# First stage of a two-layer trunk kernel in eight steps of 128 features, with x asked for first

## The chip, the core and the metric

The kernel runs on one core of a Trainium2 chip. The metric is device microseconds (us) of one execution of the whole kernel; it has one launch and no arithmetic on the host. The engines are called by their names or as the profile abbreviates them: TensorE (PE, its weight loads PEld), VectorE (DVE), ScalarE (ACT), GpSimd (POOL) and SyncE (SP), which issues most DMAs. Each engine works through its own queue in order.

## The reference

The kernel computes two layers of a streaming encoder on x of 512 tokens by 1024 features, in float32. Layer 0 mixes by retention (4 heads, 256 wide queries and keys, 512 wide values, chunks of 64), layer 1 by chunked attention (16 heads of 128). Ahead of each layer stands a normalisation with a shift, a scale and a gate that come from a conditioning vector c:

```
def rms_norm_f32(t, gain):
    return t32 * lax.rsqrt(jnp.mean(t32 * t32, axis=-1, keepdims=True) + EPS) * gain
...
m = silu(c) @ ada_w[l] + ada_b[l]         # 3 x 1024 values: shift, scale, gate
h = rms_norm_f32(x, norm_g[l]) * (1 + scale) + shift
...
proj = h @ w_in                           # layer 0: q, k, v, g in its columns
q, k = apply_rope(q, cos, sin), apply_rope(k, cos, sin) * (RET_QK_DIM ** -0.5)
o = retention(q, k, v), normalised per head, * silu(g)
x = x + gate * (o @ w_out)
```

The lines on m, h, o and x are cut to what they compute. For the change it matters that h, of 512 x 1024, needs three things: the root of the mean square of each token (a sum over all 1024 features), and one shift and one scale per feature, each a dot of 1024 products of silu(c) with a column of ada_w.

## The kernel before, in words

Matrix products are made in three passes: each operand is split in a high half (rounded to the type that TensorE multiplies) and a low half (what is left), and high x high, high x low and low x high are summed in PSUM. The split of weights is an ACT copy to the high half (`whi`, L222) and a DVE subtraction to the low half (`wlo`, L223); that of h and of others is `split` (L305 to L308). h is held with features on partitions, as `hTh` and `hTl`, in eight blocks of 128 features.

**Start.** SP asks for cond (c on all partitions), then the four tiles of x (`norm_x`, L360). Per tile `norm_rows` makes sums of squares on ACT (L168), adds them on DVE (L174), makes the root on POOL in two operations (`rstd_of`, L117 and L119) and scales the rows (L181 on DVE, for the last tile L179 on ACT). TensorE transposes the result and ACT copies it to `xT` (L369).

**First stage.** The products that the first stage makes are those of the values of head 0 (`rv0`, 512 columns of ret_w_in, four PSUM tiles `pm_rv`, one per 128 tokens) and of its queries (`rqk0_0`, 256 columns, two tiles `pm_rqk`). It runs in four steps of 256 features. `prepare(s)` asks for two 1 MB pieces of ada_w (`ada_256`), makes four dots of 1024 on DVE (L124), adds the constant parts for two features' blocks at a time (`ada_finish`), makes h on DVE (L379), splits it, and loads and splits 256 rows of the weights. The matmuls of step s come behind `prepare(s + 1)`.

**Hand-over.** Its last step is followed by the evacuation of the values (`vh` on ACT, `vl` on DVE, L306 and L307), the keys of head 0 (`rqk0_2`, weights in two halves of 512 features, `whi_rqk_2` and `wlo_rqk_2`), and the tables of sines (`rope_tables`: positions and the frequencies `tiny` are loaded through POOL's queue, the angle is made on DVE, L431 to L448). The tiles of this part lie in the pool `rp`, which is opened when the first stage's pool `st` is closed, in the same memory. `zero` (L408) is a block of zeros in it.

**The rest of layer 0.** The work is cut in units of twelve matmuls; `go` counts them in `now`, and `at(u, ...)` hangs a piece of other work behind unit u. So are the gate's eight dots hung (blocks 16 to 23 of ada_w: `side_load`, `side_dot`, L601 to L605). Behind the fourth and the eighth `ada_finish` turns four dots into 512 values of the gate: a diagonal block each (`diag`), four small matmuls that spread them to all partitions (`gp`, L146), and a copy to `gate` on ACT (L148). The output projection of head 0 (`outp`, `out_proj`) needs them: its weights `raw_r` are multiplied by a half of the gate on POOL (L219) before they are split, first half for `po_r_0`, second for `po_r_1`. `hang_scores` hangs the scores of the next head (`st`, L520).

The program is written in this order, and a scheduler with its own costs places the instructions on the engines' queues; loads and dots marked with `keep_in_program_order` keep their order among themselves. All later placing in the two kernels is the same from the second head on.

## Time and profile before

| what | us |
|---|---|
| median of three runs | 980.64 (980.63 to 984.66) |
| profiled execution | 982.98 |
| its span, from the first to the last instruction | 981.2 |
| TensorE busy | 949.3 (97%) |
| VectorE busy | 601.1 (61%) |
| ScalarE busy | 373.8 (38%) |
| GpSimd busy | 184.7 (19%) |
| mean granted clock of TensorE | 0.992 of full speed |

The span is shorter than the time of its execution by what lies around the instructions. Busy times of engines overlap. A share of the span is an average over stages: in the first of forty slices of the span TensorE is busy for three tenths, in the second for eight, and from the third on for nine or more, while the DMA engines are at nine tenths in the first slice and between two and six in nearly all others. So the stretch that the change touches is unlike the rest.

### The profile page before, as it was taken

How to read it: one execution, taken by the hardware profiler on the slowest of the kernel's cores; microseconds unless marked ns; L12 is line 12 of the kernel's file. 1: busy time of each engine (PE TensorE's matmuls, PEld its weight loads, DVE VectorE, ACT ScalarE, POOL GpSimd, SP SyncE). 2: the span in 40 equal slices, each digit the busy share in tenths (PEclk: the TensorE clock that was granted, in tenths of full speed). 3: DMA queues.
4: the chain of work that ended last, by engine and by line, in shares of the span. 5: the costliest groups of instructions: out<-in, count | busy, mean ns of one | idle time of the engine just before them, and what ended most of it. 6: DMA issues, size and time to landing. Idle time of an engine off the chain costs nothing.

```text
span 981.2 us, 11783 instructions
## 1 busy us (share of the span) xinstructions
PE 949.3 (97%) x4528; PEld 793.6 (81%) x4528; DVE 601.1 (61%) x1023; ACT 373.8 (38%) x785; POOL 184.7 (19%) x169
## 2 busy tenths in 40 slices
PE   3889999999999999999999999999999999999997
PEld 2778888888888888778788888888878888888886
DVE  4977796568544775864455557444676346555674
ACT  6233322232233233354444445233543244444441
POOL 3000520051002012503001250002520012004410
PEclk8899999999999999999999999999999999999999
DMA  9654436434443433312333213223212232223202
GB/s 352 241 191 160 149 99 204 151 108 140 150 150 108 150 100 104 97 57 80 101 97 97 79 62 103 91 87 96 97 58 93 87 97 90 79 70 99 95 1 86
DMA packets 70296, 111.76 MB, mean 114 GB/s; under 512 B 11888, under 2 KB 36512, under 8 KB 70240
## 3 DMA queue, kind: packets, MB, share of 16 engines
q1 hardware_dynamic: 58256, 103.29, 31.5%
q0 software_dynamic: 10832, 5.62, 2.1%
q10 hardware_dynamic: 1152, 2.10, 0.6%
q8 instruction: 35, 0.57, 0.2%
q14 instruction: 21, 0.17, 0.1%
HBM read 108.83 MB, written 2.10 MB: 113 GB/s over the span
## 4 chain that ended last, share of the span: by engine, by line
PE 86%; DMA 4%; issue 4%; DVE 3%; ACT 1%; POOL 1%; SPq 0%; POOLq 0%; ACTq 0%; DVEq 0%
PE pm_aqk L233 5%; PE pm_aqk L231 5%; PE pm_aqk L232 5%; PE po_a L231 3%; PE po_a L233 3%; PE po_a L232 3%; PE pm_av L232 3%; PE pm_av L233 3%; PE pm_rg L239 3%; PE pm_rg L240 3%; PE ao L765 3%; PE as L725 3%; PE pm_av L231 3%; PE pm_rg L241 3%; PE ro L540 3%
## 5 line engine op out<-in xcount | busy, mean ns | idle before, releaser
L231 PE MATMUL pm_aqk<-whi_aqk,hTh 128*128 128x512 f32 x256 | 102.3, 400 | 1.1 <-ACT hTh L200 1.1
L233 PE MATMUL pm_aqk<-whi_aqk,hTl 128*128 128x512 f32 x256 | 100.4, 393 | 0.0
L232 PE MATMUL pm_aqk<-wlo_aqk,hTh 128*128 128x512 f32 x256 | 100.2, 391 | 0.0
L124 DVE CUSTOM_DVE_ANT_0 ada<-ada,cond 128x1024 f32<-128x1024 f32 x48 | 63.3, 1332 | 1.7 <-DMA ada<-in_ada_t_dram 1.7
L219 POOL TENSOR_TENSOR raw_r<-raw_r,gate 128x2048 f32<-128x2048 f32 x8 | 38.2, 4771 | 106.3 <-DMA raw_r<-in_ret_w_out_dram 92.9
L231 PE MATMUL pm_rv<-whi_rv,hTh 128*128 128x512 f32 x128 | 51.2, 407 | 6.7 <-ACT hTh L306 6.7
L231 PEld LDWEIGHTS pm_aqk<-whi_aqk,hTh 128*128 128x128 f32 x256 | 48.1, 188 | 10.9 <-ACT hTh L200 1.5
L233 PEld LDWEIGHTS pm_aqk<-whi_aqk,hTl 128*128 128x128 f32 x256 | 48.1, 188 | 10.6 <-DVE hTl L201 0.4
L232 PEld LDWEIGHTS pm_aqk<-wlo_aqk,hTh 128*128 128x128 f32 x256 | 48.2, 188 | 9.2
L734 ACT ACTIVATE p<-p,nm 128x128 f32<-128x128 f32 (+1 forms) x64 | 35.9, 563 | 48.7 <-DVE nm L732 47.6
L223 DVE TENSOR_TENSOR wlo_aqk<-raw_aqk,whi_aqk 128x2048 fp32r<-128x2048 f32 x16 | 36.6, 2290 | 28.0 <-ACT whi_aqk L222 28.0
L728 DVE CUSTOM_DVE_ANT_0 p<-as,br 128x128 f32<-128x128 f32 (+1 forms) x64 | 30.4, 486 | 36.9 <-PE as L725 34.0
L241 PE MATMUL pm_rqk<-hTh,wlo_rqk 128*128 128x512 f32 x128 | 49.7, 391 | 2.5 <-DVE wlo_rqk L223 2.5
L713 POOL DMA_DIRECT2D br<-in_att_bias_dram x16 | 13.4, 839 | 204.4 <-DVE nm L732 168.8
L232 PE MATMUL pm_rv<-wlo_rv,hTh 128*128 128x512 f32 x128 | 50.9, 402 | 0.0
L239 PE MATMUL pm_ag<-hTh,whi_ag 128*128 128x512 f32 x128 | 50.7, 397 | 0.0
L240 PE MATMUL pm_ag<-hTl,whi_ag 128*128 128x512 f32 x128 | 50.5, 394 | 0.0
L231 PE MATMUL po_r<-whi_r,yh 128*128 128x512 f32 x128 | 49.8, 391 | 0.5 <-ACT whi_r L222 0.5
L241 PE MATMUL pm_ag<-hTh,wlo_ag 128*128 128x512 f32 x128 | 50.2, 395 | 0.0
L233 PE MATMUL po_r<-whi_r,yl 128*128 128x512 f32 x128 | 50.1, 392 | 0.0
L232 PE MATMUL po_r<-wlo_r,yh 128*128 128x512 f32 x128 | 50.0, 391 | 0.0
L231 PE MATMUL pm_av<-whi_av,hTh 128*128 128x512 f32 x128 | 50.0, 391 | 0.0
(199 smaller groups left out, 2548.6 us busy)
## 6 DMA issues: line engine op xcount, KB each, us to landing
ada<-in_ada_t_dram SPq DMA_DIRECT2D x32, 512.0 KB, 4.4
raw_aqk<-in_att_w_in_dram SPq DMA_DIRECT2D x32, 512.0 KB, 4.6
ada<-in_ada_t_dram SPq DMA_DIRECT2D x8, 1024.0 KB, 13.8
raw_rg<-in_ret_w_in_dram SPq DMA_DIRECT2D x8, 1024.0 KB, 5.1
raw_r<-in_ret_w_out_dram SPq DMA_DIRECT2D x8, 1024.0 KB, 5.0
raw_ag<-in_att_w_in_dram SPq DMA_DIRECT2D x8, 1024.0 KB, 5.2
raw_av<-in_att_w_in_dram SPq DMA_DIRECT2D x8, 1024.0 KB, 5.1
raw_a<-in_att_w_out_dram SPq DMA_DIRECT2D x8, 1024.0 KB, 4.9
```

What stands on the lines that cost most here:

```text
L124: return nc.vector.tensor_tensor_reduce(raw, raw, cond, 1.0, 0.0, ALU.mult, ALU.add, mod[:, layer, block : block + 1])
L219: nc.gpsimd.tensor_tensor(raw, raw, scale.unsqueeze(1).broadcast_to([P, k1 - k0, width]), ALU.mult)
L223: nc.vector.tensor_tensor(lo, raw, f32(hi), ALU.subtract)
L231: nc.tensor.matmul(ps, a_h, wh[:, k, :], start=first and k == 0, stop=False)
L232: nc.tensor.matmul(ps, a_h, wl[:, k, :], start=False, stop=False)
L233: nc.tensor.matmul(ps, a_l, wh[:, k, :], start=False, stop=last and k == 3)
L239: nc.tensor.matmul(ps, wh[:, k, csl], h, start=first and k == 0, stop=False)
L240: nc.tensor.matmul(ps, wh[:, k, csl], l, start=False, stop=False)
L241: nc.tensor.matmul(ps, wl[:, k, csl], h, start=False, stop=last and k == 3)
L540: nc.tensor.matmul(ps[:, S - w :], a[:, fsl], b[:, psl], start=j == 0 and z == 0, stop=j == 3 and z == 2,)
L728: nc.vector.tensor_tensor_reduce(p[:, :w], ps[:, :w], br[:, S - w :], 1.0, -3.0e38, ALU.add, ALU.max, mx)
L734: nc.scalar.activation(p[:, :w], p[:, :w], AF.Exp, bias=nm, accum_out=sm)
```

## The change

The first stage becomes eight steps of 128 features. A step asks for one 1 MB load (a block of the scale's and one of the shift's rows of ada_w) and two small ones of the first weights (512 and 256 columns of 128 rows, 256 KB and 128 KB), makes two dots on DVE, the scale on DVE and the shift on POOL, h on ACT in place of DVE, and splits it and the weights. The weights' split halves lie in whole tiles for all steps, those of the queries in the pool `st`. x is asked for first, cond behind its third tile. The sums of squares of tiles 1 and 3 are made on DVE, and the scaled rows of the last tile too. A tiny Silu at the start stands ahead of the one on cond. The loads of `rqk0_2` keep their program order. The eight dots of the gate are hung at other units.

```diff
--- before.py
+++ after.py
@@ -73,8 +73,11 @@
     pa = ctx.enter_context(tc.tile_pool(name="pa", bufs=4, space=PS))
 
     cond = cp.tile([P, D], F32, name="cond")
-    nc.sync.dma_start(cond, c_row.broadcast_to([P, D]))
     xs = [cp.tile([P, D], F32, name=f"x_{t}") for t in range(NT)]
+    for t in range(NT):
+        nc.sync.dma_start(xs[t], x[t * P : (t + 1) * P, :])
+        if t == 2:
+            nc.sync.dma_start(cond, c_row.broadcast_to([P, D]))
     ng = cp.tile([P, 2, NK], F32, name="ng")
     nc.gpsimd.dma_start(ng, norm_t)
     bt = cp.tile([P, 2, 24], F32, name="bt")
@@ -92,11 +95,15 @@
     nc.vector.memset(ones, 1.0)
     ones_r = cp.tile([P, P], F32R, name="ones_r")
     nc.vector.tensor_copy(ones_r, ones)
     nc.gpsimd.memset(mhalf, -0.5)
 
+    tick = cp.tile([P, 8], F32, name="tick")
+    nc.vector.memset(tick, 0.0)
     with tc.high_priority():
-        nc.scalar.activation(cond, cond, AF.Silu)
+        nc.scalar.activation(tick, tick, AF.Silu)
+    nc.scalar.activation(cond, cond, AF.Silu)
     kq = cp.tile([P, 1], F32, name="kq")
     nc.vector.tensor_scalar(kq, qg, kg, float(P**-0.5), ALU.mult, ALU.mult)
 
@@ -160,25 +167,25 @@
         return sums
 
 
-    def norm_rows(t, tag, scalar=False):
+    def norm_rows(t, tag, vector=False):
 
         xn, ss = [], sp.tile([P, 2], F32, tag="ss", name=f"ss_{tag}_{t}")
         for half in range(2):
             xh = np_.tile([P, 512], F32, tag="p", name=f"xn_{tag}_{t}_{half}", bufs=6)
-            nc.scalar.activation(
-                xh, xs[t][:, half * 512 : (half + 1) * 512], AF.Square,
-                accum_out=ss[:, half : half + 1],
-            )
+            src = xs[t][:, half * 512 : (half + 1) * 512]
+            if vector:
+                nc.vector.tensor_tensor_reduce(
+                    xh, src, src, 1.0, 0.0, ALU.mult, ALU.add, ss[:, half : half + 1]
+                )
+            else:
+                nc.scalar.activation(xh, src, AF.Square, accum_out=ss[:, half : half + 1])
             xn.append(xh)
         s1 = sp.tile([P, 16], F32, tag="s1", name=f"s1_{tag}_{t}")
         nc.vector.tensor_tensor(s1[:, 0:1], ss[:, 0:1], ss[:, 1:2], ALU.add)
         rs = rstd_of(s1[:, 0:1], D, 1)
         for half in range(2):
             src = xs[t][:, half * 512 : (half + 1) * 512]
-            if scalar:
-                nc.scalar.activation(xn[half], src, AF.Copy, scale=rs)
-            else:
-                nc.vector.tensor_scalar(xn[half], src, rs, None, ALU.mult)
+            nc.vector.tensor_scalar(xn[half], src, rs, None, ALU.mult)
         return xn
 
     def norm_tile(layer, t):
...
@@ -258,7 +267,7 @@
             self.w = load(
                 [(d, self.w_in[rows, c0 : c0 + d.stop - d.start]) for d, c0 in self.cols],
                 f"{self.name}_{half}", self.width, w=self.w if ks[0] else parts,
-                k0=ks[0], k1=ks[-1] + 1,
+                k0=ks[0], k1=ks[-1] + 1, pinned=self.name == "rqk0_2",
             )
 
         def unit(self, half, u, ks=range(4)):
@@ -348,54 +357,56 @@
     with tc.tile_pool(name="st", bufs=1) as st:
         xT = st.tile([P, NK, S], F32, name="xT")
 
...
+        wv = [[wp.tile([P, 4, 512], F32R, tag=a, name=f"{a}_rv0_{z}") for a in ("whi", "wlo")] for z in range(2)]
+        wq = [[st.tile([P, 4, 256], F32R, name=f"{a}_rqk0_0_{z}") for a in ("whi", "wlo")] for z in range(2)]
+        bt1 = st.tile([P, NK], F32, name="bt1")
+        nc.gpsimd.tensor_scalar(bt1, bt[:, 0, NK : 2 * NK], 1.0, None, ALU.add)
+        for t in range(NT):
+            xn = norm_rows(t, 0, t % 2 == 1)
+            for half in range(2):
+                ps = pa.tile([P, 4, P], F32, tag="pa", name=f"hp_0_{t}_{half}")
+                for k in range(4):
+                    nc.tensor.transpose(ps[:, k, :], xn[half][:, k * P : (k + 1) * P], ident)
+                nc.scalar.activation(
+                    xT[:, half * 4 : half * 4 + 4, t * P : (t + 1) * P], ps, AF.Copy
+                )
+        rows = ada_t[0, : 2 * D].rearrange("(g q p) k -> q p g k", g=2, q=NK)
+        def prepare(kt):
+            raw = st.tile([P, 2, D], F32, tag="ada", name=f"ada_0_{kt}", bufs=4)
+            tc.keep_in_program_order(nc.sync.dma_start(raw, rows[kt]))
+            rw = st.tile([P, 768], F32, tag="rw", name=f"rw_{kt}", bufs=4)
+            ksl = slice(kt * P, (kt + 1) * P)
+            nc.sync.dma_start(rw[:, :512], ret_w_in[ksl, 2 * D : 2 * D + 512])
+            nc.sync.dma_start(rw[:, 512:], ret_w_in[ksl, 0:256])
+            ada_dot(raw[:, 1, :], 0, NK + kt)
+            g1, s1 = gs[:, 0, kt : kt + 1], sh[:, 0, kt : kt + 1]
+            nc.vector.scalar_tensor_tensor(
+                g1, mod[:, 0, NK + kt : NK + kt + 1], bt1[:, kt : kt + 1], ng[:, 0, kt : kt + 1],
+                ALU.add, ALU.mult,
             )
...
+            ada_dot(raw[:, 0, :], 0, kt)
+            nc.gpsimd.tensor_tensor(s1, mod[:, 0, kt : kt + 1], bt[:, 0, kt : kt + 1], ALU.add)
+            half, k = divmod(kt, 4)
+            for (hi, lo), src in ((wv[half], rw[:, :512]), (wq[half], rw[:, 512:])):
+                split(hi[:, k, :], lo[:, k, :], src)
+            h = np_.tile([P, S], F32, tag="nat", name=f"h_0_{kt}")
+            nc.scalar.activation(h, xT[:, kt, :], AF.Identity, bias=s1, scale=g1)
+            split(hT["h"][:, kt, :], hT["l"][:, kt, :], h)
+        def products(kt):
+            for ch, w in zip(first, (wv, wq)):
+                ch.w = (None, *w[kt // 4])
+                for u in range(ch.n):
+                    ch.unit(kt // 4, u, range(kt % 4, kt % 4 + 1))
         prepare(0)
...
+        for kt in range(NK - 1):
+            prepare(kt + 1)
+            products(kt)
 
     offs = (0, 512, 896, 1152)
 
@@ -600,15 +611,14 @@
         blocks = [(0, 16 + b) for b in range(8)]
         blocks += [(1, b) for b in (*range(8, 16), *range(8), *range(16, 24))]
         for z, (layer, block) in enumerate(blocks):
-            u = 2 + 2 * z if z < 8 else 20 + (z - 8) * 7 // 2
+            u = 5 + 3 * z // 2 if z < 8 else 20 + (z - 8) * 7 // 2
             at(max(u - 4, 0), side_load, layer, block)
             at(u, side_dot, layer, block)
 
         rope_tables()
         for ch, ev in zip(first, (v_evac(0), qk_evac(0))):
             ch.evac = ev
-            for u in range(ch.n):
-                ch.unit(1, u, range(2, 4))
+        products(NK - 1)
         go(Chunk("rqk0_2", ret_w_in, [(h256, D)], True, qk_evac(0, 2)).units())
         hang_scores(0, now[0] + 2)
         for n in range(RH):
```

TensorE's queue around the last matmuls of the second gate half (`gp_20`, columns 512 to 1023 of the gate) in the kernel before. `po_r_0` and `po_r_1` are the two column halves of the first output projection, `st` the scores of the next head:

```order
L146 MATMUL gp_20_992<-diag_22_999,ones 128x128
L231 MATMUL po_r_0_0_1109<-whi_r_0_1103,yh_1_854 128x512
L232 MATMUL po_r_0_0_1109<-wlo_r_0_1104,yh_1_854 128x512
L146 MATMUL gp_20_992<-diag_23_1002,ones 128x128
L233 MATMUL po_r_0_0_1109<-whi_r_0_1103,yl_1_855 128x512
L231 MATMUL po_r_0_0_1109<-whi_r_0_1103,yh_2_893 128x512
...
L520 MATMUL st_1_1182<-qh_1_1053,kl_1_1098 128x384
L231 MATMUL po_r_1_0_1200<-whi_r_1_1194,yh_0_818 128x512
L520 MATMUL st_2_1214<-qh_0_1048,kh_0_1092 128x256
...
L231 MATMUL po_r_1_1_1225<-whi_r_1_1194,yh_0_818 128x512
...
L231 MATMUL po_r_1_2_1252<-whi_r_1_1194,yh_0_818 128x512
L232 MATMUL po_r_1_0_1200<-wlo_r_1_1195,yh_0_818 128x512
```

And in the changed kernel:

```order
L242 MATMUL po_r_0_3_1205<-whi_r_0_1140,yl_3_973 128x512
L153 MATMUL gp_20_1016<-diag_20_1017,ones 128x128
L531 MATMUL st_0_1194<-qh_0_1085,kh_0_1129 128x512
L153 MATMUL gp_20_1016<-diag_21_1020,ones 128x128
...
L531 MATMUL st_2_1251<-qh_1_1090,kl_1_1135 128x256
L153 MATMUL gp_20_1016<-diag_22_1023,ones 128x128
L153 MATMUL gp_20_1016<-diag_23_1026,ones 128x128
L531 MATMUL st_3_1278<-qh_0_1085,kh_0_1129 128x256
...
L531 MATMUL st_3_1278<-qh_1_1090,kl_1_1135 128x256
L240 MATMUL po_r_1_0_1237<-whi_r_1_1231,yh_0_854 128x512
...
L240 MATMUL po_r_1_3_1304<-whi_r_1_1231,yh_0_854 128x512
L241 MATMUL po_r_1_0_1237<-wlo_r_1_1232,yh_0_854 128x512
```

In before the last `gp_20` stands inside the first unit of `po_r_0`; now it stands behind the whole of `po_r_0` and the first three blocks of scores, and the first `po_r_1`, with `whi_r_1`, is seven instructions behind it.

ScalarE's queue at the end of the first stage in the kernel before, with the semaphores that each instruction waits for; `vh` is the high half of the values, `whi_rqk_2_0` the first half of the keys' weights:

```order
L306 ACTIVATE hTh_111<-h_7_401 128x512 [waits DVE_49]
L306 ACTIVATE vh_490<-pm_rv_0_277 128x512 [waits DMAHW6_49,DMAHW5_49,DMAHW7_49,DMAHW0_49,PE_49]
L306 ACTIVATE vh_490<-pm_rv_1_284 128x512 [waits PE_49]
L306 ACTIVATE vh_490<-pm_rv_2_291 128x512 [waits PE_49]
L306 ACTIVATE vh_490<-pm_rv_3_298 128x512 [waits PE_49]
L222 ACTIVATE whi_rqk_2_0_549<-raw_rqk_2_0_548 128x4x256 [waits DMAHW5_49,Activation_49]
L222 ACTIVATE whi_rqk_2_1_588<-raw_rqk_2_1_587 128x4x256 [waits DMAHW0_49,DVE_49,PE_49]
```

And in the changed kernel:

```order
L315 ACTIVATE hTh_118<-h_7_480 128x512 [waits Activation_49]
L315 ACTIVATE vh_542<-pm_rv_0_268 128x512 [waits DMAHW2_49,DMAHW7_49,DVE_49,PE_49]
L315 ACTIVATE vh_542<-pm_rv_1_272 128x512
L315 ACTIVATE vh_542<-pm_rv_2_276 128x512
L315 ACTIVATE vh_542<-pm_rv_3_280 128x512
L231 ACTIVATE whi_rqk_2_0_586<-raw_rqk_2_0_585 128x4x256 [waits DMAHW5_49]
L231 ACTIVATE whi_rqk_2_1_622<-raw_rqk_2_1_621 128x4x256 [waits DMAHW0_49]
```

The first `vh` waits for loads, DVE and TensorE in the changed kernel, since its memory is that of the first stage's pool; the PE event is that of the last matmul of the first stage. The other copies and the keys' weights stand behind it.

GpSimd's queue at the same place in the kernel before:

```order
L119 TENSOR_TENSOR rs<-ms,mhalf 128x1 [waits Pool_49]
L423 DMA posi<-in_positions_dram 128x512 [waits DVE_49]
L408 MEMSET zero 128x128 [waits DMAHW5_49,DMAHW2_49,DMAHW6_49,DMAHW1_49,DMAHW7_49,DMAHW0_49,DVE_49]
L426 DMA tiny<-in_inv_freq_dram 128x1
L427 MEMSET tiny 128x1
```

And in the changed kernel:

```order
L392 TENSOR_TENSOR sh<-mod,bt 128x1 [waits DVE_49] x8
L434 DMA posi<-in_positions_dram 128x512 [waits Activation_49]
L419 MEMSET zero 128x128 [waits DMAHW3_49,DMAHW2_49,DMAHW4_49,DMAHW1_49,DMAHW5_49,DMAHW0_49,DMAHW6_49,DVE_49,DMAHW7_49,PE_49,Activation_49]
L437 DMA tiny<-in_inv_freq_dram 128x1
L438 MEMSET tiny 128x1
```

The block of zeros, which is written into the same memory, now waits for TensorE and ScalarE too, and the load of the frequencies `tiny` stands behind it in both.

## Rows read from the trace of the kernel before

**Rows 1.** The page's busy table, whole span: busy us, share, instructions.
```profile
PE 949.3 (97%) x4528; PEld 793.6 (81%) x4528; DVE 601.1 (61%) x1023; ACT 373.8 (38%) x785; POOL 184.7 (19%) x169
```

**Rows 2.** Waits of TensorE, whole span: line waited for: us in total, times, longest.
```profile
PE pm_rv L231 <- ACT hTh L306: 6.7, 2, 4.0
```

**Rows 3.** Timeline of TensorE: start, us, line, operation, shape, count, idle before.
```profile
17.20 2.21 PE L368 MATMUL hp<-ident,xn 128*128 128x128 f32 x8 [2.63 <-ACT xn L179]
23.42 0.80 PE L231 MATMUL pm_rv<-whi_rv,hTh 128*128 128x512 f32 x1 [4.01 <-ACT hTh L306]
...
62.34 0.39 PE L239 MATMUL pm_rqk<-hTh,whi_rqk 128*128 128x512 f32 x1
...
65.94 0.50 PE L241 MATMUL pm_rqk<-hTh,wlo_rqk 128*128 128x512 f32 x1 [2.52 <-DVE wlo_rqk L223]
...
71.51 0.39 PE L241 MATMUL pm_rqk<-hTh,wlo_rqk 128*128 128x512 f32 x1
```

**Rows 4.** Timeline of VectorE, the start and the first step (same columns).
```profile
9.20 0.88 DVE L181 TENSOR_SCALAR xn<-x,rs 128x512 f32<-128x512 f32 x2 [0.98 <-POOL rs L119]
...
13.48 0.15 DVE L174 TENSOR_TENSOR s<-ss 128x1 f32<-128x1 f32 x1
...
25.42 1.22 DVE L124 CUSTOM_DVE_ANT_0 ada<-ada,cond 128x1024 f32<-128x1024 f32 x1
...
26.57 0.69 DVE L307 TENSOR_TENSOR hTl<-h,hTh 128x512 fp32r<-128x512 f32 x1
27.17 1.22 DVE L124 CUSTOM_DVE_ANT_0 ada<-ada,cond 128x1024 f32<-128x1024 f32 x1
```

**Rows 5.** Timeline of GpSimd, root for the last tile of x.
```profile
14.97 1.42 POOL L119 TENSOR_TENSOR rs<-ms,mhalf 128x1 f32<-128x1 f32 x1
```

**Rows 6.** Timeline of ScalarE at the end of the first stage.
```profile
59.82 0.60 ACT L306 ACTIVATE vh<-pm_rv 128x512 fp32r<-128x512 f32 x1 [0.76 <-PE pm_rv L233]
60.32 1.05 ACT L222 ACTIVATE whi_rqk<-raw_rqk 128x1024 fp32r<-128x1024 f32 x1
```

**Rows 7.** Windows: stretch, us, busy per engine, TensorE's clock, DMA share, GB/s.
```profile
16.90:27.00 10.10, 5.79 (x17) 4.25 (x17) 7.91 (x15) 6.72 (x11) 0.00 (x0) 0.50 1.04 417
...
44.50:47.50 3.00, 3.00 (x7) 2.42 (x8) 3.00 (x6) 1.49 (x3) 0.00 (x0) 0.50 0.00 0
...
63.40:66.00 2.60, 0.07 (x2) 0.06 (x1) 2.60 (x5) 0.00 (x0) 0.00 (x0) 1.00 0.00 0
```

**Rows 8.** DMA issues, first 70 us: count, KB each, median us to landing.
```profile
ada<-in_ada_t_dram SPq DMA_DIRECT2D x8, 1024.0 KB, 13.8
...
kg<-in_att_kg_t_dram POOLq DMA_DIRECT2D x1, 0.5 KB, 5.6
tiny<-in_inv_freq_dram POOLq DMA_DIRECT2D x1, 0.5 KB, 7.0
```

**Rows 9.** Timeline of VectorE, angle and second low weights.
```profile
56.16 0.49 DVE L431 TENSOR_SCALAR ang<-posf,tiny 128x512 f32<-128x512 f32 x1
...
59.06 0.43 DVE L440 TENSOR_SCALAR n<-ang 128x512 f32<-128x512 f32 x1
...
64.66 1.22 DVE L223 TENSOR_TENSOR wlo_rqk<-raw_rqk,whi_rqk 128x1024 fp32r<-128x1024 f32 x1
```

**Rows 10.** Timeline of GpSimd, gate times raw_r.
```profile
105.37 5.59 POOL L219 TENSOR_TENSOR raw_r<-raw_r,gate 128x2048 f32<-128x2048 f32 x1 [1.39 <-ACT gate L148]
...
135.56 4.69 POOL L219 TENSOR_TENSOR raw_r<-raw_r,gate 128x2048 f32<-128x2048 f32 x1 [11.95 <-ACT gate L148]
```

**Rows 11.** Timeline of TensorE, last matmuls of the second gate half.
```profile
134.46 0.38 PE L146 MATMUL gp<-diag,ones 128*128 128x128 f32 x2
```

**Rows 12.** Timeline of ScalarE, gate and high half.
```profile
134.88 0.60 ACT L148 ACTIVATE gate<-gp 128x512 f32<-128x512 f32 x1 [3.34 <-PE gp L146]
...
141.38 1.90 ACT L222 ACTIVATE whi_r<-raw_r 128x2048 fp32r<-128x2048 f32 x1
```

**Rows 13.** Timeline of VectorE, low half.
```profile
146.19 2.28 DVE L223 TENSOR_TENSOR wlo_r<-raw_r,whi_r 128x2048 fp32r<-128x2048 f32 x1
```

More of the change, by code (lines that the diff above doesn't have):

```diff
@@ L94, in hybrid_trunk_kernel @@
     nc.vector.tensor_copy(ones_r, ones)
-    mhalf = cp.tile([P, 40], F32, name="mhalf")
+    mhalf = cp.tile([P, 32], F32, name="mhalf")
     nc.gpsimd.memset(mhalf, -0.5)
+    tick = cp.tile([P, 8], F32, name="tick")
+    nc.vector.memset(tick, 0.0)
     with tc.high_priority():
-        nc.scalar.activation(cond, cond, AF.Silu)
+        nc.scalar.activation(tick, tick, AF.Silu)
+    nc.scalar.activation(cond, cond, AF.Silu)
     kq = cp.tile([P, 1], F32, name="kq")
@@ L201, in norm_tile, with load @@
             nc.vector.tensor_tensor(hT["l"][:, ksl, tsl], h, f32(hT["h"][:, ksl, tsl]), ALU.subtract)
-    def load(parts, name, width=512, scale=None, w=None, k0=0, k1=4):
+    def load(parts, name, width=512, scale=None, w=None, k0=0, k1=4, pinned=False):
         if w is None:
@@ L349, in hybrid_trunk_kernel @@
         xT = st.tile([P, NK, S], F32, name="xT")
-        def ada_256(b0):
-            raw = st.tile([P, 2, D], F32, tag="ada", name=f"ada_0_{b0}", bufs=6)
-            nc.sync.dma_start(
-                raw, ada_t[0, b0 * P : (b0 + 2) * P, :].rearrange("(b p) k -> p b k", p=P)
-            )
-            for j in range(2):
-                ada_dot(raw[:, j, :], 0, b0 + j)
-            ada_finish(0, b0, 2)
-        def norm_x():
-            for t in range(NT):
-                nc.sync.dma_start(xs[t], x[t * P : (t + 1) * P, :])
-            for t in range(NT):
-                xn = norm_rows(t, 0, t == 3)
-                for half in range(2):
-                    ps = pa.tile([P, 4, P], F32, tag="pa", name=f"hp_0_{t}_{half}")
-                    for k in range(4):
-                        nc.tensor.transpose(ps[:, k, :], xn[half][:, k * P : (k + 1) * P], ident)
-                    nc.scalar.activation(
-                        xT[:, half * 4 : half * 4 + 4, t * P : (t + 1) * P], ps, AF.Copy
-                    )
@@ L373, in prepare @@
-        def prepare(s):
-            ada_256(NK + 2 * s)
-            ada_256(2 * s)
-            for kt in (2 * s, 2 * s + 1):
-                h = np_.tile([P, S], F32, tag="nat", name=f"h_0_{kt}")
-                nc.vector.tensor_scalar(
-                    h, xT[:, kt, :], gs[:, 0, kt : kt + 1], sh[:, 0, kt : kt + 1], ALU.mult, ALU.add
-                )
-                split(hT["h"][:, kt, :], hT["l"][:, kt, :], h)
-            for ch in first:
-                ch.load(s // 2, ks(s))
-        def ks(s):
-            return range(s % 2 * 2, s % 2 * 2 + 2)
@@ L389, in hybrid_trunk_kernel @@
-        norm_x()
-        prepare(0)
-        for s in range(3):
-            ws = [ch.w for ch in first]
-            prepare(s + 1)
-            for ch, w in zip(first, ws):
-                new, ch.w = ch.w, w
-                for u in range(ch.n):
-                    ch.unit(s // 2, u, ks(s))
-                ch.w = new
+        wv = [[wp.tile([P, 4, 512], F32R, tag=a, name=f"{a}_rv0_{z}") for a in ("whi", "wlo")] for z in range(2)]
+        wq = [[st.tile([P, 4, 256], F32R, name=f"{a}_rqk0_0_{z}") for a in ("whi", "wlo")] for z in range(2)]
@@ L609, in hybrid_trunk_kernel @@
             ch.evac = ev
-            for u in range(ch.n):
-                ch.unit(1, u, range(2, 4))
+        products(NK - 1)
         go(Chunk("rqk0_2", ret_w_in, [(h256, D)], True, qk_evac(0, 2)).units())
```

4 lines of the change are left out of this document (3 added, 1 removed).

## Prediction, made before the changed kernel was timed

> **What bounds the kernel now.** I read the busy table first: TensorE is busy for 949.3 us of the span [rows 1], so a change pays only by removing TensorE's idle time, and costs only by adding some. Then the list of TensorE's waits, and TensorE's timeline over the first 150 us to see where these waits lie. The reader is to see two things. The idle time that this change can reach lies ahead of 66 us: after the transposes of x the first matmul comes at 23.42, 4.01 late; a second wait for h takes the other 2.7 us of its 6.7, and a third gap of 2.52 ends at 65.94, when the low half of the third weights is ready [rows 2, 3]. The first stage is over at 62.34, when the next chunk's first matmul starts [rows 3]. Of the 32 us that TensorE is idle in all, the start and these gaps are most, so behind 66 us there is little slack: whatever the first stage gains reaches the end of the kernel unless a new wait eats it.
>
> Sums are made against the profiled execution (982.98, its span 981.2, so 1.8 around it); it is 2.34 above the median of the runs, 980.64. I apply differences to the median. Half a per cent, 4.9 us, is what a measurement here can tell from no change: 975.74 and 985.54 are the bounds.
>
> **The start.** x is asked for ahead of cond, and two of the four sums of squares move to VectorE. The last tile still goes through GpSimd, whose two tiny operations run beside VectorE's dots: in before the sum of its squares is there at 13.48 and its root at 14.97 + 1.42 = 16.39 [rows 4, 5]. I leave that chain where it is, since x's last tile arrives behind the same bytes as before. Then the two scaled halves (0.88 for two [rows 4], 17.3), transposes and the copy to xT (four transposes, half of the 2.21 of the last eight [rows 3], and a copy of 0.6 [rows 6]: 1.7), then h and its high half on ScalarE at 0.6 each [rows 6]: 20.2 for the first matmul, 3.2 ahead of 23.42. What goes is that four dots had to be over before h; now two have.
>
> **The eight steps.** A step is 18 matmuls. At the full clock they start 0.227 apart (24 from 65.94 to 71.51, the first of them 0.11 slow [rows 3]), so 4.08 a step. VectorE in a step: two dots 1.15 apart, three low halves (two of 512 at 0.60, one of 256, half of that), a small one of 0.1 [rows 4]: 2.3 + 1.5 + 0.1 = 3.9. ScalarE: h, its high half and two weights, 2.2. GpSimd: one small addition, which I bound by nothing and by 1.42, the worst of its small operations beside dots [rows 5]; it is hidden, as the steps are prepared one ahead. Loads: 1.44 MB at the 417 GB/s of the stretch from 16.9 to 27 [rows 7] is 3.4. So TensorE sets the pace and the gap of 2.7 in the middle, with its 3.0 us at half clock behind it [rows 7], goes. The half clock at the start stays: it lasted from 23.42 to 27.0 [rows 3, 7]. End of the stage: 20.2 + 3.6 (eight and a half matmuls) + 135.6 x 0.227 = 54.6, against 62.34: 7.7 earlier.
>
> **The hand-over gives part of it back.** The small weights of all eight steps now lie in the pool whose memory the next stage reuses, so the first copy of v and GpSimd's zero block wait for the last matmul of the stage, as the order shows. In before the four copies of v lay beside matmuls. Now: four copies 0.5 apart and then the high weights, 1.05 [rows 6], TensorE idle from 54.6 to about 57.95, with 0.2 for the release. Queued behind GpSimd's zero block is the load of the frequencies: issued at 54.95, landing 5.6 to 7.0 later (the shortest and this load's own in before [rows 8]). VectorE's angle operation waits for it, and the second low weights stand behind five operations of the angle: 3.3 in before, from 56.16 to 59.49, then 1.15 to 1.22 [rows 9]. They are ready at 65.0 to 66.4, I take 65.7. TensorE gets to their first use 28 matmuls after 57.95 plus a short wait for the first low half: 64.6 at the full clock, 66.1 with 3.0 us at half clock as after the gap of 2.7 [rows 7]. That gap of 2.52 was followed by full clock [rows 7], this one is 3.35, so I take the half: 66.1. In before the same matmul starts at 71.51 [rows 3]. What is left is 5.4 us; ends 4.9 and 6.9.
>
> **The second half of the gate.** The unit numbers of the eight gate dots change, and with them the place at which the last matmul of the second gate half stands. In before it starts at 134.46; the gate is copied from 134.88, GpSimd scales raw_r from 135.56 for 4.69, the high half starts at 141.38 and takes 1.90, the low half 146.19 and 2.28, done at 148.47 [rows 10 to 13]. TensorE did not notice, because 55 instructions of the output projection and the scores stand between the gate's last matmul and the first that needs the high half, and 14 more ahead of the first that needs the low half. In the changed kernel all of the first projection half stands ahead of the gate; behind it stand only six matmuls of st_3 (256 columns, 0.12 each, half of a 512-column one) and four that need the high half. From the start g of the gate's last matmul: copy at g + 0.42, GpSimd g + 1.1 to 5.8, high half g + 5.9 to 7.8 (in before 1.1 after GpSimd's end, behind another copy), low half to g + 10.1. The matmul that needs it would stand at g + 1.8 without a wait: 8.3 us lost. The low end is 6.0 (if only the wait for the high half counted, 7.8 less 1.8), the high end 9.2: GpSimd took 0.9 longer in the first half of the gate [rows 10]. TensorE stands still for 7.0 of that, so the clock falls; half clock lasted 3.0 and 3.6 us [rows 3, 7], which costs 1.5 to 1.8, of which up to two thirds lie in the shadow of the wait for the low half: 0.5 to 1.7, I take 1.1. Nothing makes this good later, as from there on the order of all engines is the same as before.
>
> Sum: -5.4 + 8.3 + 1.1 = +4.0, so 984.6 (987.0 for the profiled execution).
>
> **Rivals.** (C) The loads become the pace, and it is slower. Each load waits for the landing of the one eight ahead; eight are 2.67 steps, 10.9 us at TensorE's pace. If they take longer than that to land, TensorE waits at every step. For it: the loads of the shift and scale rows took 13.8 us to land [rows 8]. Against it: that was queueing at 417 GB/s with 256 KB loads among them [rows 7, 8], and less is outstanding now. At 13.8 a step takes 5.2, the stage ends at 61.8, and the hand-over takes the rest: 71.51 is missed by about 1.8, so nothing gained and the gate's 9.4 lost, 980.64 + 9.4 = 990.0, or 991.8 at worst. The Trainium skill bears on this one ("DMA: Bandwidth & Descriptors", section "Measured (HBM→SBUF, 128 partitions, SWDGE, issued from GpSimd)"): it says to batch DMAs to at least 1 MiB for 75% of peak, with 341 GB/s for 1 MB against 138 for 64 KB. By it the 384 KB that come in two loads per step would take up to 2.8 us and the 1 MB 3.1, an estimate of 5.9 per step, slower than TensorE. The trace disagrees as far as it goes: 417 GB/s with loads of 256 KB, 512 KB and 1 MB queued together.
>
> (B) The gate's wait isn't there, because something ahead of it on TensorE already waits, or the gap is filled: only the 5.4 stay, 975.3. For it: in before the whole chain lay hidden. Against it: the durations of GpSimd, ScalarE and VectorE [rows 10, 12, 13] leave nothing to choose, TensorE's queue is in order.
>
> (D) The hand-over costs less (the load lands in 5.6 and the clock holds) and the gate's wait has no clock loss behind it: -6.9 + 8.3 = +1.4, 982.0.
>
> **Numbers.** Forecast 0.66, 984.6, its own range 982 to 988; C 0.14, B 0.10, D 0.10. Slower by over 0.5%: 0.25 of the forecast and 0.11 of C, 0.36. Within: 0.41, 0.09 of D, 0.03 of B and 0.03 of C, 0.56. Faster: 0.07 of B and 0.01 of D, 0.08. The range of 8 in 10 leaves out B and the worst of C: 980.0 to 989.5.
>
> **What would show it.** First matmul at 19.5 to 20.7 and no gap before 54; a gap of 3.3 at 54.6 ended by ScalarE's high weights; TensorE at the first use of the second low weights at about 66; one gap of some 7 us near 142 on the first po_r matmul of the second half, released by whi_r, and half clock behind it; after that the same timeline shifted by 4. It is wrong if GpSimd's scaling lies beside TensorE work, if steps take over 4.3 us, or if idle time appears behind 160 us.

## The result, and the profile after: 994.15 us, slower by 1.1%

The median of the changed kernel's runs is 994.15 us (991.99 to 995.03), that of the kernel before on the same chip 981.14: a ratio of 1.0108, interval 1.0086 to 1.0129. Forecast were 984.6 and a range of 980.0 to 989.5. The quotient of these two medians, of four runs each, would be 1.0133; the text goes by ratios with their intervals, and a second chip gave 1.0111. The profiled execution took 995.01, its span 993.2 against 981.2.

TensorE's busy time in the page of the changed kernel, beside [rows 1]: it rose by 6.5 us though the matmuls are the same, since part of them ran at half clock.

```profile
PE 955.8 (96%) x4528; PEld 798.9 (80%) x4528; DVE 599.8 (60%) x1030; ACT 376.9 (38%) x792; POOL 189.1 (19%) x178
```

Its list of TensorE's waits (us in total, times, longest), beside [rows 2]:

```profile
PE po_r L240 <- ACT whi_r L231: 8.0, 2, 6.2
PE ss L164 <- POOL sq L561: 4.3, 1, 4.3
PE pm_rqk L248 <- ACT whi_rqk L231: 3.1, 1, 3.1
PE pm_rv L240 <- ACT hTh L315: 2.7, 1, 2.7
```

The wait for h is down to one of 2.7. The waits of 6.2 and 3.1 were forecast; the one of 4.3 for the sums of squares was not. The other 1.8 of the first line stands at 427.8; the kernel before waits 0.5 at the same place. TensorE's timeline of the changed kernel shows where they lie, beside [rows 3]:

```profile
20.06 0.80 PE L240 MATMUL pm_rv<-whi_rv,hTh 128*128 128x512 f32 x1 [2.67 <-ACT hTh L315]
...
58.50 0.50 PE L248 MATMUL pm_rqk<-hTh,whi_rqk 128*128 128x512 f32 x1 [3.09 <-ACT whi_rqk L231]
...
71.28 0.39 PE L248 MATMUL pm_rg<-hTh,whi_rg 128*128 128x512 f32 x1
...
128.76 1.11 PE L164 MATMUL ss<-ident,sq 128*128 128x128 f32 x4 [4.25 <-POOL sq L561]
...
157.66 2.07 PE L240 MATMUL po_r<-whi_r,yh 128*128 128x512 f32 x4 [6.20 <-ACT whi_r L231]
159.99 0.80 PE L241 MATMUL po_r<-wlo_r,yh 128*128 128x512 f32 x1 [0.25 <-DVE wlo_r L232]
```

The first stage did what was forecast: first matmul at 20.06 (20.2 forecast, 23.42 before), no gap up to the end of the stage at 55.41. The first matmul of rg comes at 71.28; before it came at 76.04. Then two gaps with half clock behind each. The changed kernel's windows (stretch, us, busy per engine, clock, DMA) beside [rows 7]:

```profile
36.00:40.00 4.00, 4.00 (x19) 3.34 (x18) 4.00 (x9) 2.31 (x5) 0.57 (x1) 1.00 1.03 393
...
58.50:62.00 3.50, 3.50 (x9) 2.49 (x10) 3.36 (x7) 0.90 (x1) 0.00 (x0) 0.63 0.34 55
...
124.00:128.00 4.00, 0.51 (x3) 0.09 (x1) 4.00 (x3) 0.69 (x2) 3.92 (x2) 0.96 0.43 137
128.00:132.00 4.00, 3.24 (x10) 2.75 (x11) 4.00 (x7) 0.00 (x0) 0.71 (x1) 0.50 0.74 265
132.00:136.00 4.00, 4.00 (x14) 3.16 (x13) 4.00 (x9) 1.23 (x2) 1.84 (x1) 0.69 0.24 95
152.00:156.00 4.00, 0.00 (x0) 0.00 (x0) 4.00 (x1) 0.82 (x4) 4.00 (x2) 0.87 0.00 0
156.00:160.00 4.00, 2.08 (x5) 1.17 (x5) 3.58 (x6) 3.41 (x2) 0.51 (x1) 0.50 0.15 34
160.00:164.00 4.00, 4.00 (x14) 3.26 (x15) 3.62 (x4) 0.00 (x0) 0.00 (x0) 0.77 0.70 191
```

The sums cost 4.25 idle, 3.24 x 0.5 = 1.6 and 4 x 0.31 = 1.2 at a lower clock: 7.1. The second gate half costs 6.45 idle, 2.08 x 0.5 = 1.0 and 4 x 0.23 = 0.9: 8.4.

GpSimd's timeline of the changed kernel tells why the sums are late (beside the first row of [rows 10]); `dec` is the decay tile of the second head:

```profile
108.11 0.81 POOL L517 DMA_DIRECT2D dec<-in_decay_dram  x1 [42.23 <-DVE pf L536]
116.26 0.15 POOL L518 MEMSET dec<- 64x64 f32 x1 [7.34 <-DMA dec<-in_decay_dram]
116.56 4.96 POOL L228 TENSOR_TENSOR raw_r<-raw_r,gate 128x2048 f32<-128x2048 f32 x1 [0.15 <-POOL dec L518]
121.49 7.22 POOL L561 TENSOR_TENSOR sq<-sq,sq 128x512 f32<-128x512 f32 x3
```

And the same place in the kernel before:

```profile
103.17 0.81 POOL L506 DMA_DIRECT2D dec<-in_decay_dram  x1 [41.63 <-DVE pf L525]
105.37 5.59 POOL L219 TENSOR_TENSOR raw_r<-raw_r,gate 128x2048 f32<-128x2048 f32 x1 [1.39 <-ACT gate L148]
113.04 0.15 POOL L507 MEMSET dec<- 64x64 f32 x1 [2.08 <-DMA dec<-in_decay_dram]
113.27 5.38 POOL L550 TENSOR_TENSOR sq<-sq,sq 128x512 f32<-128x512 f32 x3
```

TensorE's first sum in the kernel before, which waits for nothing:

```profile
119.92 0.60 PE L157 MATMUL ss<-ident,sq 128*128 128x128 f32 x4
```

The zero block is written into the tile that the load fills, so it waits for the load, which lands 8 to 10 us after its issue. In before the scaling of the first gate half lay in that time; in the changed kernel the zero block stands ahead of it. The gate was copied at 110.49, so the scaling was held up for some 5 us behind a block of 64 x 64. The gate itself came later too (its copy starts at 104.69 in before); that alone does not make the sums wait, as a run below shows.

### The profile page after: what moved, and what is told of

Same layout as the page of the kernel before. It is cut to its first block, busy times and chain, and to the rows that moved or that the text cites. A ratio compares the mean times of both kernels' runs of the same rounds, so it can differ in the third digit from the quotient of the medians.

```text
span 993.2 us, 11827 instructions
## 1 busy us (share of the span) xinstructions
PE 955.8 (96%) x4528; PEld 798.9 (80%) x4528; DVE 599.8 (60%) x1030; ACT 376.9 (38%) x792; POOL 189.1 (19%) x178
## 4 chain that ended last, share of the span: by engine, by line
PE 89%; DMA 3%; issue 2%; POOL 2%; DVE 2%; ACT 1%; SPq 0%; POOLq 0%; DVEq 0%; ACTq 0%
PE pm_aqk L242 6%; PE pm_aqk L240 6%; PE pm_aqk L241 6%; PE as L735 3%; PE ao L775 3%; PE pm_rv L240 3%; PE pm_rv L241 3%; PE po_a L240 3%; PE pm_rv L242 3%; PE pm_rg L250 3%; PE po_a L242 3%; PE po_a L241 3%; PE pm_av L241 3%; PE pm_av L240 3%; PE pm_av L242 3%; PE pm_rg L248 3%
## 5 line engine op out<-in xcount | busy, mean ns | idle before, releaser
L131 DVE CUSTOM_DVE_ANT_0 ada<-ada,cond 128x1024 f32<-128x1024 f32 x48 | 66.4, 1394 | 3.5 <-DMA ada<-in_ada_t_dram 3.5
L248 PE MATMUL pm_rqk<-hTh,whi_rqk 128*128 128x512 f32 x128 | 50.7, 407 | 3.1 <-ACT whi_rqk L231 3.1
L738 DVE CUSTOM_DVE_ANT_0 p<-as,br 128x128 f32<-128x128 f32 (+1 forms) x64 | 30.4, 486 | 36.9 <-PE as L735 34.0
L249 PE MATMUL pm_rqk<-hTl,whi_rqk 128*128 128x512 f32 x128 | 51.7, 404 | 0.0
```

Source lines behind the costliest of these rows:

```text
L131: return nc.vector.tensor_tensor_reduce(raw, raw, cond, 1.0, 0.0, ALU.mult, ALU.add, mod[:, layer, block : block + 1])
L248: nc.tensor.matmul(ps, wh[:, k, csl], h, start=first and k == 0, stop=False)
L249: nc.tensor.matmul(ps, wh[:, k, csl], l, start=False, stop=False)
L738: nc.vector.tensor_tensor_reduce(p[:, :w], ps[:, :w], br[:, S - w :], 1.0, -3.0e38, ALU.add, ALU.max, mx)
```

## The experiments

One measure serves for all: the start of a matmul less 0.2275 us for each 512 columns of matmuls ahead of it in that kernel's order. I call it lag; it grows with idle time and half clock, and a little with small matmuls, which start further apart than their columns say. It is worked out from each kernel's one trace, at the first matmuls of rg and at some 200 us of work, behind the second gate half. The kernel before gains 2.0 between the two, with no wait on the way.

| kernel | ratio to before (interval) | first matmul | lag at rg | behind the gate |
|---|---|---|---|---|
| before | 1 | 23.42 | 30.5 | 32.5 |
| changed | 1.0108 (1.0086 to 1.0129) | 20.06 | 26.2 | 44.1 |
| changed, again | 1.0111 (1.0094 to 1.0129) | 20.89 | 26.9 | 44.9 |
| before, new units | 1.0051 (1.003 to 1.0071) | 23.44 | 30.8 | 39.8 |
| changed, zero block behind | 1.0074 (1.0048 to 1.0101) | 20.11 | 26.5 | 41.3 |
| changed, old units | 1.0072 (1.0044 to 1.0099) | 20.21 | 30.2 | 39.2 |
| changed, units 2z | 1.0016 (1.0 to 1.0032) | 20.32 | 32.0 | 34.3 |
| changed, units 5 to 10 | 0.999 (0.9977 to 1.0003) | 20.16 | 25.3 | 29.8 |
| changed, units 5 to 12 | 1.0044 (1.0029 to 1.0058) | 20.31 | 25.5 | 34.8 |
| early load | 1.0059 (1.0037 to 1.0081) | 21.23 | 26.4 | 33.5 |
| early load, old units | 1.0056 (1.0034 to 1.0078) | 22.07 | 32.4 | 36.7 |
| early load, units 5 to 12 | 0.9985 (0.997 to 0.9999) | 20.99 | 26.9 | 28.9 |
| early load, zero block behind | 0.9988 (0.9978 to 0.9999) | 22.35 | 28.8 | 30.6 |
| before, x first | 0.9995 (0.9981 to 1.0009) | 22.80 | 31.7 | 33.7 |
| hand-over swapped | 1.0031 (1.0016 to 1.0046) | 21.68 | 30.4 | 34.4 |

The changed kernel run again on a second chip:

> The changed kernel as it is, beside the others on this chip, as their common measure: a ratio of 1.009 to 1.013 to the kernel before, with the waits of 4.2 for the sums of squares and 6.2 for the second gate weights. If the ratio is below 1.007, the runs on the other chip overstated the loss.

It came out so, with the waits of 4.25 and 6.20.

**The unit numbers alone, in the kernel before.**

```diff
-            u = 2 + 2 * z if z < 8 else 20 + (z - 8) * 7 // 2
+            u = 5 + 3 * z // 2 if z < 8 else 20 + (z - 8) * 7 // 2
```

> The kernel before with nothing but the new unit numbers of the eight gate dots. The order then has the gate's last matmul where it was (as many matmuls ahead of the second projection half), but GpSimd's zero block ahead of the scaling of the first gate half. Theory 1 (it is GpSimd's order that makes the sums late): a wait of 1 to 4 us for the sums with half clock behind it, 983 to 986, and no wait for the second gate weights. The prediction's own step (the unit numbers move the gate's last matmul and cost 9.4): 990. Rival (the zero block is ready early enough in this kernel, where the load is issued at the same place): no change, 981.

> The kernel before with the new unit numbers, once more for its trace, since the profiled execution of the first time was disturbed. If GpSimd's order is what costs (the timed runs were 0.5% above before), the trace shows the zero block waiting for its load ahead of the scaling of the first gate half, the scaling starting 4 to 6 us later than in before, and a wait of TensorE for the sums of squares of 1 to 4 us; at the second gate half no wait. If instead the gate's place is what costs, the wait stands at the second gate weights.

0.5% slower, and the trace (988.61 against 982.72 on that chip) has one new wait. TensorE's and GpSimd's timelines of this kernel:

```profile
124.42 1.11 PE L157 MATMUL ss<-ident,sq 128*128 128x128 f32 x4 [4.04 <-POOL sq L550]
```

```profile
113.01 0.15 POOL L507 MEMSET dec<- 64x64 f32 x1 [8.71 <-DMA dec<-in_decay_dram]
113.31 5.49 POOL L219 TENSOR_TENSOR raw_r<-raw_r,gate 128x2048 f32<-128x2048 f32 x1 [0.15 <-POOL dec L507]
118.75 5.61 POOL L550 TENSOR_TENSOR sq<-sq,sq 128x512 f32<-128x512 f32 x3
```

The wait for the sums comes without any new first stage, and the second gate half has no wait. So the unit numbers swap GpSimd's order, and in this kernel they do not move the second gate half: the prediction's cause for that move is wrong.

**The zero block put behind the scaling, in the changed kernel.**

```diff
-            nc.gpsimd.memset(dec[64:128, 0:64], 0.0)
+            if n == 1:
+                nc.gpsimd.tensor_scalar(dec[64:128, 0:64], scaled[0][64:128, 0, 0:64], 0.0, None, ALU.mult)
+            else:
+                nc.gpsimd.memset(dec[64:128, 0:64], 0.0)
```

> The changed kernel with one edit: the zero block of the second head's decay tile is written as a scaled first half of the gate times zero, so that on GpSimd it can stand only behind that scaling and no longer ahead of it. Theory 1 (in the changed kernel the scaling waits behind the zero block, which waits for a decay load; TensorE's wait of 4.25 for the sums of squares and the half clock behind it come from this order): the scaling starts at about 111.2 instead of 116.56, the wait for the sums is gone, and of the 7.5 lost there 6.5 to 7.5 come back: 986.6 to 987.7. The second wait, for the high half of the second gate weights, stays at about 6 us. Rival (the sums are late because the gate's last matmul stands later on TensorE, and GpSimd would be late in any order): the wait for the sums stays at over 3 us, 993 to 995.

The wait for the sums is gone and the scaling starts at 111.53, but the lag behind the gate falls by 2.8, not by 7, and the time by less than theory 1 said. TensorE gets as far as 128.75 and then waits for the next thing, VectorE's second rope, in this kernel's timeline:

```profile
130.59 0.47 PE L243 MATMUL po_r<-whi_r,yh 128*128 128x512 f32 x1 [1.84 <-DVE rt L480]
```

VectorE was busy for all of 116 to 132 us there: a gate dot lies between the parts of the rope, and two dots ahead of it took 2.3 us beside GpSimd's work where the dot behind them took 1.2. Neither theory had that.

**Other unit numbers in the changed kernel.** Only the formula differs: `2 + 2 * z`, `2 * z`, `(5, 6, 7, 8, 8, 9, 9, 10)[z]`, `5 + z`.

> The changed kernel with the unit numbers of the eight gate dots as they were before. The order then has GpSimd's scaling ahead of the zero block again, and the gate's last matmul 26 rows (5.9 us at the full clock) further ahead on TensorE. Theory 1 (both late waits come from the order that the unit numbers helped to set): the wait for the sums goes (-7.5), the wait for the second gate weights shrinks from 6.4 to 0.5 to 3 us with less half clock behind it (-4.5 to -7): 980 to 982. Theory 2 (the wait for the sums comes from the first stage itself, which ends earlier and so meets the decay load): the wait for the sums stays, 988 to 990.

> The changed kernel with the unit numbers of the eight gate dots at twice their index, earlier than in either kernel. The order then has the gate's last matmul 76 rows further ahead, GpSimd's scaling ahead of the zero block, and at the hand-over two more of VectorE's dots ahead of the angle operations. Theory 1 (the two late waits are all that takes the gain of the first stage): both go, -7.5 and -8.4 from 994.2; the dots ahead of the angles make the second low weights 3 to 4 us late for TensorE, with half clock behind: 980 to 984. Rival (a wait that is taken away is paid later by another, since the engines behind TensorE are full there): 987 or more.

Both lost the whole gain at the hand-over, more than I had expected, and not to the dots. The loads of the dots are asked for four units ahead, on the queue of the third weights. The second half of these weights was asked for at 38.03 in the changed kernel; with `2 * z` it was asked for at 63.19, behind two loads of dots. ScalarE's timeline with `2 * z`:

```profile
69.48 1.06 ACT L231 ACTIVATE whi_rqk<-raw_rqk 128x1024 fp32r<-128x1024 f32 x1 [10.64 <-DMA raw_rqk<-in_ret_w_in_dram]
```

TensorE waited 4.17 for it there, and 3.02 with the old numbers. So the changed kernel's larger numbers keep the hand-over short, at the price of everything behind it. With `2 * z` neither late wait is left; with the old numbers the sums don't wait and the gate waits 4.03.

> The changed kernel with the unit numbers 5, 6, 7, 8, 8, 9, 9, 10 for the eight gate dots: the first dot at the same unit as in the changed kernel, the last five units earlier. The order then keeps VectorE's angle operations ahead of all dots at the hand-over, as in the changed kernel, and has the gate's last matmul 95 rows (21 us at the full clock) ahead of the first that needs the second gate weights, against 7 in the changed kernel; the diagonals of the second gate half stand ahead of the second rope on VectorE, as in the kernel before. Theory 1 (the first stage and the hand-over keep 4.4 us; all the loss comes from dots, diagonals and scalings that VectorE and GpSimd do too late between 100 and 160 us): neither wait is left, the time is 3 to 6 us below before, a ratio of 0.994 to 0.997. Rival (VectorE is full between 70 and 150 us in any order, so earlier dots make something else late): 1.000 or more.

> The changed kernel with the unit numbers 5 to 12, one apart. The gate's last matmul stands 50 rows (11 us) ahead of the first that needs its weights, but the diagonals of the second gate half stand behind the second rope on VectorE, as in the changed kernel. Theory 1 (the distance on TensorE decides, and 9.9 us are needed from the gate's last matmul to the low half): no wait or one below 1 us at the second gate half, a ratio of 0.995 to 0.999. Theory 2 (VectorE's order decides, with the diagonals late behind the rope): TensorE waits for the diagonals ahead of the gate by 2 us or more, 1.000 to 1.004.

With 5 to 10 the hand-over is as in the changed kernel, and neither wait is there: only 0.56 and 0.99 for yl and yh. The lag at the gate is 2.7 below before, but the time only 0.1% (within noise), so the range of theory 1 was missed; in this one trace three small waits behind 390 us that before's trace lacks (0.73, 1.24, 0.67) take back 2.6 us. With 5 to 12 the distance on TensorE was not enough: 0.86 for the diagonals, 1.14 for yl, 0.98 for VectorE's additions to x, and 1.69 for the low half of the second gate weights. The high half of these was over at 143.42, but VectorE got to the low half at 147.76: it decides there, as theory 2 had it, though the wait for the diagonals is 0.86 and not 2. More than order is in it: that yl, 0.7 elsewhere, took 5.07 beside GpSimd's scaling of 5.53.

**The 512 bytes of the frequencies loaded at the start**, instead of behind the zero block at the hand-over:

```diff
     nc.gpsimd.dma_start(kg, att_kg_t)
+    tiny = cp.tile([P, 2], F32, name="tiny")
+    nc.gpsimd.dma_start(tiny[:, 0:1], inv_freq)
+    nc.gpsimd.memset(tiny[:, 1:2], math.pi / 2)
```

> The changed kernel with one edit: the 512 bytes of the frequencies are loaded at the very start into memory of their own, no longer at the hand-over behind GpSimd's zero block. The unit numbers are those of the changed kernel. The order then starts VectorE's angles ahead of the copies of v, and has the gate's second half where the kernel before has it (69 matmuls ahead of the first that needs its high half), but on GpSimd the zero block of the second head still stands ahead of the scaling of the first gate half. Theory 1 (two separate causes: the gate's place comes from the hand-over, the wait for the sums of squares from the zero block ahead of the scaling): the wait for the second gate weights is gone, that for the sums stays at 3 to 5 us, a ratio of 1.001 to 1.005. Rival (both waits have one cause, VectorE's lateness after the hand-over): both go, 0.996 or less.

With the change's own unit numbers the order has the second gate half where it was in before, and its wait is gone; the sums wait 3.40. Two causes, as theory 1 had it; the time is slightly above its range.

> The changed kernel with the early load of the frequencies and the unit numbers of before as well. The order then has the gate's second half and GpSimd's scaling where the kernel before has them, with the new first stage in front. Theory 1 (the new first stage is worth 4 us, and all of the loss is order behind it): no wait for the sums or the second gate weights, a ratio of 0.994 to 0.998. Rival (the first stage's gain is lost again in any order, since VectorE is full up to 150 us): 0.999 or more.

> The changed kernel with the early load of the frequencies and unit numbers 5 to 12. GpSimd's scaling is ahead of the zero block, the gate's last matmul 96 rows ahead of the first that needs its high half, and VectorE has one dot less ahead of the second low weights at the hand-over than with the unit numbers of before. Theory 1: as for the run with the unit numbers of before, 0.993 to 0.997. Rival: dots closer together push the ropes back and small waits for yh and yl come in their place, as with the numbers 5 to 10 without the early load, 0.998 to 1.000.

The old numbers fail again: 1.44 for the late third weights, and 2.19 for the sums, although the scaling now stands ahead of the zero block. Its GpSimd timeline:

```profile
108.24 5.56 POOL L231 TENSOR_TENSOR raw_r<-raw_r,gate 128x2048 f32<-128x2048 f32 x1
120.04 0.15 POOL L518 MEMSET dec<- 64x64 f32 x1 [6.24 <-DMA dec<-in_decay_dram]
120.26 4.32 POOL L561 TENSOR_TENSOR sq<-sq,sq 128x512 f32<-128x512 f32 x3
```

The load took 12.7 us from its issue at 107.37, and the squares stood behind the zero block. Units 5 to 12 with the early load are the lowest ratio found: no wait between 60 and 390 us, 0.9985, though its interval nearly touches 1. The range of theory 1 was missed here too. The time is the rival's, but the small waits that the rival named are not there: the lag behind the gate is 3.6 below before, and the time 1.5 us. Where the other 2 us go is not shown.

**Both causes taken away**, with the change's own unit numbers (the last two edits together):

> The changed kernel with its own unit numbers and two edits together: the early load of the frequencies, and the second head's zero block written so that it stands behind GpSimd's scaling and the first product of the squares. Theory 1 (two causes, the gate's place and the zero block's, and nothing else): alone the first gave 1.006 with a wait of 3.4 for the sums left; that wait and the 2.3 us of half clock behind it now go too, a ratio of 0.998 to 1.001. Rival (the zero block is only the last of several late things, and another operation of GpSimd or VectorE makes the sums or the output projection late instead): 1.003 or more, with a new wait of over 1.5 us between 115 and 130 us.

0.9988: theory 1. The two edits lower the time by 12 us (1.0111 less 0.9988, times 983), all of the 11 that the changed kernel lost and 1 more, though the first matmul comes 1.5 to 2.3 us later. No difference to the version before this one (0.9985) can be told. No wait stands where the sums waited; this kernel's windows:

```profile
116.00:120.00 4.00, 4.00 (x22) 3.31 (x21) 3.21 (x4) 0.72 (x1) 0.79 (x1) 1.00 0.39 131
120.00:124.00 4.00, 4.00 (x19) 3.33 (x18) 3.90 (x10) 1.92 (x1) 1.96 (x1) 1.00 0.51 163
124.00:128.00 4.00, 4.00 (x22) 3.36 (x21) 4.00 (x6) 0.00 (x0) 0.00 (x0) 1.00 0.65 162
```

The rope's wait of 1.84 is gone too: VectorE is not late any more.

**x first, alone, in the kernel before** (the loads of x moved ahead of cond, with cond behind the third):

> The kernel before with x asked for ahead of cond (cond behind its third tile) and nothing else. Theory of the prediction (x's last tile arrives behind the same bytes, and the first matmul waits for the dots that need cond): the first matmul within 0.7 us of 23.42, a ratio of 0.999 to 1.001. Rival (x first is what made the first matmul 3.4 us earlier): it comes at 20 to 21, 0.997 to 0.998.

The first matmul moves by 0.6, the time not at all. So the 3 us at the start do not come from x's place. That they come from the dots, as the prediction said, fits but was not tried by itself.

**The hand-over**, on the version with the lowest ratio: the first half of the third weights loaded and split ahead of the last step's products, pinned ahead of the copies of v (`keys.load(0)` ahead of `products(NK - 1)`, with `tc.keep_in_program_order` on these, on the copies of v and on the first rope's products).

> The kernel with the early load and unit numbers 5 to 12 (0.9985), with one thing more: the third high weights and their low half are made ahead of the copies of v, on ScalarE and VectorE, as the order shows; the first copy of v still waits for the last matmul of the stage, and the next chunk's result takes the place of the first v, so TensorE must wait for one copy and its low half. Theory 1 (the prediction's: the gap of 3.6 at the hand-over is four copies of v and the weights in line on ScalarE): the gap falls to 1.5 to 2.3 us with half clock behind it, and 1.5 to 2.5 us are gained, a ratio of 0.996 to 0.998. Rival (the second low weights, now behind the whole first rope on VectorE, come later by what the gap has lost): a second gap of 1 to 2 us behind it, 0.998 to 1.000.

It failed, and tests neither theory: the gap grew from 3.61 to 5.54. ScalarE's timeline:

```profile
58.41 0.63 ACT L460 ACTIVATE sin<-ang 128x512 f32<-128x512 f32 x1 [11.52 <-DVE ang L459]
58.95 0.71 ACT L462 ACTIVATE cos<-n,tiny 128x512 f32<-128x512 f32 x1
59.56 1.04 ACT L234 ACTIVATE whi_rqk<-raw_rqk 128x1024 fp32r<-128x1024 f32 x1
60.51 2.04 ACT L321 ACTIVATE vh<-pm_rv 128x512 fp32r<-128x512 f32 x4
```

The edit also put sin and cos ahead of the weights. They wait for the angle, which on VectorE stands behind two casts of GpSimd's zero block, which waits for the last matmul. Whether the swap alone pays stays open.

## Why the prediction was wrong

**The step that failed is one that it left out.** It followed one of the two scalings of the gate. It forecast "one gap of some 7 us near 142"; there are two, and the first, at the sums, which the sum put at nothing, cost 7.1 more. Its own sentence, "whatever the first stage gains reaches the end of the kernel unless a new wait eats it", asked for every engine's order to be read against the one before; GpSimd's was read at the hand-over only. There the zero block stands ahead of the scaling, and the row above shows that the load behind it lands 8 to 10 us after its issue. In before the squares ended at 113.27 + 5.38 = 118.65, and the first sum started at 119.92 without a wait, 1.3 us later: some 5 us of delay could not stay hidden. The run of the unit numbers alone shows the cause, and the one with both edits that nothing else of size is missing.

**A cause was wrong.** "The unit numbers of the eight gate dots change, and with them the place at which the last matmul of the second gate half stands": in before they leave it where it was; with the early load it goes back under the new numbers. What moves it is the order chosen behind the new hand-over, with the small load in it; the numbers shift it from there. The sum did not suffer, since the place itself was read off the order.

**The second gate half** was right as a mechanism: forecast 8.3 + 1.1, measured 6.45 idle and 1.9 of half clock by these windows, 1.0 less than forecast. It lies some 10 us later than forecast (151.4 to 157.66, not "near 142"). The gate's last matmuls at 149.85, the scaling 4.50 at 151.17, the high half 1.91 at 155.70 answer to [rows 10 to 12].

**The first stage** was right: 4.08 a step, no gap, and the stage over at 55.41 where 54.6 was forecast.

**The hand-over** was right in its gap (3.35 forecast, 3.09 measured), wrong in what follows: the frequencies landed 2.2 us after their issue, where [rows 8] gave 5.6 to 7.0; the second low weights came at 64.1, not 65.7, and did not bind. The gain was 4.8 at the first matmul of rg, and 4.4 by 100 us, where 5.4 was forecast. The half clock that the prediction chose is in the rows: 0.63 from 58.5 to 62.

Sum: -4.4 + 7.1 + 8.4 = 11.1 of the 12.0 between the spans. By lag the two stretches come to 15.9 (44.1 less 26.2, less the 2.0 of before) and not 15.5; the other 0.5 lies elsewhere. Forecast were -5.4 + 9.4 = +4.0. Of the miss of 8, 7.1 is the wait for the sums and 1.0 the smaller gain; the gate came out up to 1.0 lower, and the 0.9 that this leaves has no place in the sum.

**Rival C** (loads set the pace) fell: the loads land as these rows say, at 393 GB/s in the window shown, and no step waited. The margin was small: 1.44 MB at 393 GB/s are 3.7 us of a step of 4.08. The changed kernel's DMA issues, beside [rows 8]:

```profile
ada<-in_ada_t_dram SPq DMA_DIRECT2D x8, 1024.0 KB, 10.9
...
rw<-in_ret_w_in_dram SPq DMA_DIRECT2D x8, 256.0 KB, 10.9
rw<-in_ret_w_in_dram SPq DMA_DIRECT2D x8, 128.0 KB, 8.9
...
tiny<-in_inv_freq_dram POOLq DMA_DIRECT2D x1, 0.5 KB, 2.2
```
The Trainium skill's rule on loads of 1 MiB ("DMA: Bandwidth & Descriptors", "Measured (HBM→SBUF, 128 partitions, SWDGE, issued from GpSimd)") stands on a rate for each size of load, measured with loads issued from GpSimd. For loads of 128 KB to 1 MB that SyncE queued together this trace disagrees: 393 GB/s in all.

**Rivals B and D** fell too. The gate's wait was there, against B. The frequencies did land early (2.2 us), as D had it, but the clock fell behind both gaps, to 0.63 in the window at the hand-over and 0.50 in the one at the gate.

## What to carry to other kernels

Where an instruction waits for a load on an engine that works in order, look at what stands behind it: a block of 64 x 64 held back a scaling, the squares, the sums and TensorE. When a change makes a stage shorter, compare the order of every engine at every later place where the slack was small, not only at the one that moved most; each microsecond of such a wait cost 0.3 to 0.7 more in half clock. And a small load at the right time can be worth more than the stage: 512 bytes asked for early and one block put later lowered the time by 12 us. The first stage's own gain did not all reach the end: where no wait of size was left behind it, lag was 2 to 4 us below before, and the time 1 to 1.5.
